# A convolution mixer with seven-product matmuls: the small sums of f's weights on GpSimd behind the next pair's sums, the convolution's second step behind an addition, one Silu a product later

## The chip, the cores and the metric

The kernel runs on one core of one Trainium2 chip. The metric is the device time of one execution in microseconds (us); lower is better. The kernel before took 827.8 us (median of 3 runs, 826.64 to 828.01).

## What is computed

The reference is one layer (DEPTH is 1) of a streaming encoder with a gated short-convolution mixer. The input x is 1024 tokens by 1024 channels in float32, the inner width is 2048.

```python
def short_conv_mixer(u, w_in, conv_w, w_out):
    z, bg, cg, v = jnp.split(u @ w_in.astype(u.dtype), 4, axis=-1)
    y = bg * causal_dwconv(cg * v, conv_w) * jax.nn.silu(z)
    return y @ w_out.astype(u.dtype)
...
    u = rms_norm(h, pre_norm[i])
    m = short_conv_mixer(u, ...)
    h = h + rms_norm(m, post_norm[i])
```

`w_in` is 1024 x 8192 (four blocks of 2048 columns: z, bg, cg, v), the convolution is causal with 3 taps for each channel, `w_out` is 2048 x 1024. The SSD mixer of the reference's file is not used at this depth.

## The kernel before, in words

**The work and its order.** The inner width is cut into 16 chunks of 128 channels (`c`, 0 to 15). A chunk has two pairs of weight blocks: pair 2c is (cg, v), pair 2c+1 is (z, bg). For one pair the projection of all 1024 tokens is a 2 x 2 block product (two weight blocks by two halves of the tokens, and the contraction in two halves), and it is done with seven products `a` to `g` in the place of eight, on sums and differences of the weights (`add_s`: the sums `se`, `sc`, `sf` and, in place, d's; GpSimd) and of the activations (`UH`, `UL`). Each fp32 operand is split into a high and a low part (`wah` and `wal` for the weights of a), and each product is three matmuls for each of four blocks of the contraction: 12 matmuls of 128 x 512. The high part is a copy on ScalarE, the low part a subtraction on VectorE; `split_by_bank` lets ScalarE put a second copy of the source in a PSUM bank (`beside`) and VectorE read that one.

From chunk 3 on product b, and in the chunks 4 to 14 (`by_seven("f", c)`) product f as well, are themselves done by seven smaller products of 128 x 256 (`a'` to `g'`) over both pairs of the chunk at once. Their weights are sums again: `deep_sums(z, c, part)` makes four steps of 128 x 256 in two pages (`dsf0`: lines L730 and L731, `dsf1`: lines L733 and L734 for f; `dsb` for b). `dwf1h`, `dwf1l` are the split parts of `dsf0`, `dwf2h`, `dwf2l` those of `dsf1`.

The products of a chunk of 4 to 14 stand in this order (`slots`): for the even pair c, e, then a', b' of b, d, then a', b' of f, a of the odd pair, c', e' of b, g of the even pair; for the odd pair c, c' and e' of f, e, then f' of b, f' of f, d' of b, d' of f, d, g' of b, g' of f, a of the next chunk's even pair, and last g. TensorE's c adds to the PSUM bank in which a stands, g to the one in which d was added; so c waits until a was copied out of the bank (`snap`, L229, ScalarE), and g until d was added to a page (L248, VectorE).

**What follows a product** is emitted right behind it (`after`, `deep_after`, `deep_after_f`), and `prepare` splits weights about 7 us ahead of their product by a list of nominal times. Each engine runs its instructions in the order in which they were emitted; a step that waits holds up all that stand behind it on its engine. Pages for weights, sums and snapped results come from one ring of 36.

**The convolution** of a chunk starts when d' of b has been added (L783): the gate's product into `gpad` (L271, VectorE), the first tap on ScalarE (L655, into `cv`), the second and the third tap on VectorE (`conv_tap`, L661). After the odd pair's d, `sne` (L248) gets the third part of its sum, and GpSimd multiplies it by the second half of `cv` (L252). After g' of b the page `sna` of the odd pair goes through Silu (L1007, ScalarE), and the Silu of `snc` (L798) follows g' of f. After the odd pair's g VectorE multiplies the first half of `cv` by the bank and by `sna` (L264, L265), and SyncE writes `cv` to DRAM (`y_d`).

**Beside these** VectorE makes sums for the second projection: `add_t` on `w_out` (L342 and L329 to L337, chunks 4 to 11) and `add_y` on finished chunks (L294 in chunks up to 8; from chunk 9 on L299 to L301, which read an earlier chunk that SyncE fetches back, `s<-y_d`). SyncE issues all these DMAs in one queue.

Of the kernel before, what the change touches and what calls it, by code (L numbers as in the profile page):

```python
# [23 lines left out]
def kernel(  # L24
# [16 lines left out]
    nc = tc.nc  # L41
# [194 lines left out]
    def after(p, i):  # L236
# [9 lines left out]
        elif i == "d":  # L246
            t = sn[p, "e"]
            nc.vector.tensor_add(t, x_, t)  # L248
            if p == len(PAIRS) - 1:
                conv_tap(c, TAPS - 1)  # L250
# [18 lines left out]

    def start_conv(c, beside=lambda: None):  # L270
        nc.vector.tensor_mul(gpad[:, TAPS - 1 : TAPS - 1 + HB], banks[2 * c, "x"], sn[2 * c, "a"])  # L271
        conv(c, beside)
# [378 lines left out]

    def conv(c, beside=lambda: None):
        cv = tmp.tile([P, L], F32, tag="cv", name=f"cv_{c}")
        cvs[c] = cv
        nc.scalar.activation(cv, gpad[:, :L], AF.Copy, scale=tap(c, 0))  # L655
        beside()
        for j in range(1, TAPS - (c == NC - 1)):
            conv_tap(c, j)
# [64 lines left out]
    def deep_sums(z, c, part):  # L723

        eng = nc.gpsimd if z == "b" else nc.vector
        (a11, a12), (a21, a22) = rows_of(z, c)
        t = page(f"ds{z}{part}_{c}")
        deep[z, c, part] = t
        if part == 0:
            eng.tensor_add(t[:, :HH], a21, a22)  # L730
            eng.tensor_sub(t[:, HH:], t[:, :HH], a11)  # L731
        else:
            eng.tensor_sub(t[:, :HH], a11, a21)  # L733
            eng.tensor_sub(t[:, HH:], a12, deep[z, c, 0][:, HH:])  # L734
# [45 lines left out]
    def deep_after(c, i):  # L780
        which, row, half = DEEP_C[i]
        t = sn[2 * c + row, "a"][:, half * HH : (half + 1) * HH]
        nc.vector.tensor_add(t, banks[c, "b" + which][:, :HH], t)  # L783
        if i == "d'":
            start_conv(c, lambda: third_unit(1) if c == NC - 1 else None)

    def deep_after_f(c, i):
# [14 lines left out]
        if i == "d'":  # L802
            both = t1.rearrange("p (a b) -> p a b", a=2)
            nc.vector.tensor_add(both, ps.unsqueeze(1).broadcast_to([P, 2, HH]), both)
            return
# [187 lines left out]
    for n, slot in enumerate(slots):  # L993
        if slot[2:]:
# [7 lines left out]
            if i == "e'" and by_seven("f", c):  # L1002
                deep_sums("f", c, 1)
            elif (i, c) == ("f'", NC - 1):
                third_unit(0)
            elif i == "g'":
# [4 lines left out]
        if i == "a" and p % 2 and f7:  # L1011
            deep_sums("f", p // 2, 0)
# [16 lines left out]
        elif i == "e":  # L1029
            add_s(q, "ecdf" if f7 else "ec")  # L1030
            if p % 2 and q in TODO:
# [19 lines left out]
        elif i == "a":  # L1051
            if p % 2 and p in TODO:
                add_t(TODO[p], [2, 3])
# [262 lines left out]
```

## Time and profile before

| | |
|---|---|
| three runs | 826.64, 827.8, 828.01 us |
| the profiled execution | 826.64 us, its span 824.8 us |
| granted TensorE clock, mean | 0.989 |
| TensorE (PE) busy | 783.6 us, 95% |
| VectorE (DVE) busy | 696.9 us, 84% |
| ScalarE (ACT) busy | 400.5 us, 49% |
| GpSimd (POOL) busy | 354.1 us, 43% |

The profile is of one execution. Rows of the timeline give the start, the duration, the engine, the line, what is written and read, and in brackets how long the engine had been idle before and what ended that; where VectorE's steps follow each other directly, the next starts some 0.07 us before the shown end of the last. Rows of the waits read: engine, waiting line, releaser, us in total, how often, the longest. The chunks 4 to 14 lie between about 155 and 650 us of the span: 238 to 360 us are chunks 5 to 7, 500 to 650 us chunks 12 to 14.

### The profile page before, as it was taken

What the parts mean: (1) busy time and instruction counts of PE and PEld (TensorE: products, weight loads), DVE (VectorE), ACT (ScalarE), POOL (GpSimd) and SP (SyncE); (2) the same over time, 40 slices, a digit from 0 to 9 for tenths busy, and PEclk for the clock granted to TensorE, in tenths of its full rate; (3) what the DMA queues carried; (4) which work ended last, traced back from release to release, by engine and by line L of the source; (5) the groups of instructions that cost most, each with busy time, mean ns of one, the idle gap of its engine ahead of it and who ended that gap; (6) DMA issues with size and microseconds to landing.
All of it is one profiled execution on the core that took longest, in us unless ns stands there. A gap on an engine that the chain in (4) does not pass through costs nothing.

```text
span 824.8 us, 11904 instructions
## 1 busy us (share of the span) xinstructions
PE 783.6 (95%) x4050; PEld 665.1 (81%) x4050; DVE 696.9 (84%) x1008; ACT 400.5 (49%) x742; POOL 354.1 (43%) x293
## 2 busy tenths in 40 slices
PE   8999999998999999999897989999999999999997
PEld 7888888887877777778686877888888889988985
DVE  6899658879898989898888888788888899996875
ACT  7654435353535353535263434545554556855730
POOL 2425679685444444444333352535454310430031
PEclk9999999998999999999999999999999999999999
DMA  9112240625162626262737363414141979876445
GB/s 317 42 51 73 68 140 1 192 73 176 57 217 87 221 85 219 85 219 87 228 103 237 115 199 102 141 52 141 52 141 52 314 272 361 303 248 212 153 147 186
DMA packets 115822, 127.18 MB, mean 154 GB/s; under 512 B 7416, under 2 KB 74032, under 8 KB 115760
## 3 DMA queue, kind: packets, MB, share of 16 engines
q1 hardware_dynamic: 115744, 126.41, 47.3%
q8 instruction: 32, 0.52, 0.3%
q14 instruction: 30, 0.25, 0.1%
q10 hardware_dynamic: 16, 0.00, 0.0%
HBM read 91.78 MB, written 34.60 MB: 153 GB/s over the span
## 4 chain that ended last, share of the span: by engine, by line
PE 37%; DVE 20%; issue 8%; ACT 5%; DMA 3%; POOL 1%; DVEq 0%; POOLq 0%; SPq 0%; ACTq 0%
PE px L221 4%; PE po_x L1105 4%; PE po_x L1107 4%; PE po_x L1106 4%; PE px L222 3%; PE px L223 3%; DMA s<-y_d 3%; ACT beside L182 1%; DVE t L342 1%; DVE sne L248 1%; DVE dsf L734 1%; DVE sna L783 1%; DVE snc L807 1%; PE pv L222 1%; PE pv L221 1%
## 5 line engine op out<-in xcount | busy, mean ns | idle before, releaser
L252 POOL TENSOR_TENSOR sne<-sne,cv 128x512 f32<-128x512 f32 x15 | 20.9, 1396 | 153.1 <-DVE sne L248 137.9
L221 PE MATMUL px<-u_c,wcl 128*128 128x512 f32 x124 | 52.1, 420 | 20.6 <-ACT sna L229 20.6
L661 DVE SCALAR_TENSOR_TENSOR cv<-gpad,cw,cv 128x1024 f32<-128x1024 f32 x32 | 42.8, 1338 | 18.4 <-ACT cv L655 17.8
L152 POOL TENSOR_TENSOR se<-raw,raw 128x512 f32<-128x512 f32 x31 | 44.1, 1422 | 31.1 <-DVE t L334 12.8
L221 PE MATMUL px<-u_g,wgl 128*128 128x512 f32 x124 | 49.7, 401 | 5.9 <-DVE sne L248 5.9
L187 DVE TENSOR_TENSOR wel<-se,weh 128x512 fp32r<-128x512 f32 x31 | 37.6, 1213 | 19.1 <-ACT weh L168 19.1
L182 ACT COPY beside<-raw 128x512 f32<-128x512 f32 x66 | 38.9, 590 | 30.0 <-DVE dwf0l L183 14.5
L222 PE MATMUL px<-u_c,wch 128*128 128x512 f32 x124 | 51.0, 411 | 0.0
L223 PE MATMUL px<-u_c,wch 128*128 128x512 f32 x124 | 51.0, 411 | 0.0
L154 POOL TENSOR_TENSOR sc<-se,raw 128x512 f32<-128x512 f32 x31 | 46.6, 1503 | 8.4 <-POOL se L152 4.1
L156 POOL TENSOR_TENSOR sf<-raw,sc 128x512 f32<-128x512 f32 x31 | 48.6, 1567 | 1.8 <-DVE dsf L734 1.0
L221 PE MATMUL px<-u_d,wdl 128*128 128x512 f32 x124 | 48.6, 392 | 0.0
L221 PE MATMUL px<-u_a,wal 128*128 128x512 f32 x124 | 48.6, 392 | 0.0
L222 PE MATMUL px<-u_g,wgh 128*128 128x512 f32 x124 | 48.5, 392 | 0.0
L222 PE MATMUL px<-u_a,wah 128*128 128x512 f32 x124 | 48.5, 391 | 0.0
L222 PE MATMUL px<-u_d,wdh 128*128 128x512 f32 x124 | 48.5, 391 | 0.0
L222 PE MATMUL pv<-u_e,weh 128*128 128x512 f32 x124 | 48.4, 390 | 0.0
L223 PE MATMUL px<-u_d,wdh 128*128 128x512 f32 x124 | 48.4, 390 | 0.0
L221 PE MATMUL pv<-u_e,wel 128*128 128x512 f32 x124 | 48.4, 390 | 0.0
L223 PE MATMUL px<-u_g,wgh 128*128 128x512 f32 x124 | 48.3, 389 | 0.0
L223 PE MATMUL pv<-u_e,weh 128*128 128x512 f32 x124 | 48.3, 389 | 0.0
L221 PEld LDWEIGHTS px<-u_c,wcl 128*128 128x128 f32 x124 | 24.8, 200 | 29.1 <-ACT sna L229 24.0
(534 smaller groups left out, 2741.3 us busy)
## 6 DMA issues: line engine op xcount, KB each, us to landing
raw<-in_sc_w_in SPq DMA_DIRECT2D x128, 256.0 KB, 4.3
y_d<-cv SPq DMA_DIRECT2D x16, 512.0 KB, 2.9
s_d<-s SPq DMA_DIRECT2D x32, 256.0 KB, 4.5
t<-in_sc_w_out SPq DMA_DIRECT2D x32, 256.0 KB, 3.2
t_d<-t SPq DMA_DIRECT2D x32, 256.0 KB, 2.4
tb<-in_sc_w_out SPq DMA_DIRECT2D x16, 256.0 KB, 4.0
s<-y_d SPq DMA_DIRECT2D x16, 256.0 KB, 4.6
xr<-in_x SPq DMA_DIRECT2D x16, 256.0 KB, 4.5
```

The source lines that it names most:

```text
L152: nc.gpsimd.tensor_add(t, block(p, 1, 0), block(p, 1, 1))
L154: nc.gpsimd.tensor_sub(t, sums[p, "e"], block(p, 0, 0))
L156: nc.gpsimd.tensor_sub(t, block(p, 0, 1), sums[p, "c"])
L182: nc.scalar.copy(b, src)
L187: nc.vector.tensor_sub(lo, source(p, i), hi.bitcast(F32))
L221: nc.tensor.matmul(ps, lo, UH[i][:, k], start=first and k == 0, stop=False, skip_group_check=True)
L222: nc.tensor.matmul(ps, hi, UL[i][:, k], start=False, stop=False, skip_group_check=True)
L223: nc.tensor.matmul(ps, hi, UH[i][:, k], start=False, stop=last, skip_group_check=True)
L661: nc.vector.scalar_tensor_tensor(cvs[c], gpad[:, j : j + L], tap(c, j), cvs[c], op0=ALU.mult, op1=ALU.add)
L1105: nc.tensor.matmul(ps, lo, u[:, 0, k], start=first, stop=False, skip_group_check=True)
L1106: nc.tensor.matmul(ps, hi, u[:, 1, k], start=False, stop=False, skip_group_check=True)
L1107: nc.tensor.matmul(ps, hi, u[:, 0, k], start=False, stop=last, skip_group_check=True)
```

## The change

Three edits and what follows from the first, all for the chunks 4 to 14:

1. `deep_sums` for f runs on GpSimd, as for b, and both parts stand behind e of the even pair, right behind the sums of the odd pair's weights (`add_s(q, "ecdf")`). Before, part 0 stood ahead of the odd pair's a, part 1 behind e' of b, both on VectorE.
2. The convolution is cut up. Behind d' of b stand the gate's product and the first tap only; the second tap follows the addition of d' of f, and the third tap the addition of the odd pair's d (L248).
3. The Silu of `sna` moves from behind g' of b to behind a of the next chunk (after the snap of that a).
4. Since the pages of `dsf0` and `dsf1` are taken from the ring earlier, the pages behind them shift by two places.

```diff
--- before.py
+++ after.py
@@ -246,7 +246,7 @@
         elif i == "d":
             t = sn[p, "e"]
             nc.vector.tensor_add(t, x_, t)
-            if p == len(PAIRS) - 1:
+            if p == len(PAIRS) - 1 or p % 2 and by_seven("f", c):
                 conv_tap(c, TAPS - 1)
             if p % 2:
                 nc.gpsimd.tensor_mul(t, t, cvs[c][:, HB:])
@@ -267,8 +267,11 @@
             elif c < DEEP:
                 start_conv(c)
 
+    def gate(c):
+        nc.vector.tensor_mul(gpad[:, TAPS - 1 : TAPS - 1 + HB], banks[2 * c, "x"], sn[2 * c, "a"])
+
     def start_conv(c, beside=lambda: None):
-        nc.vector.tensor_mul(gpad[:, TAPS - 1 : TAPS - 1 + HB], banks[2 * c, "x"], sn[2 * c, "a"])
+        gate(c)
         conv(c, beside)
 
 
@@ -649,10 +652,12 @@
     add_s(2, "ecdf")
     fetch(3)
 
+    def first_tap(c):
+        cvs[c] = tmp.tile([P, L], F32, tag="cv", name=f"cv_{c}")
+        nc.scalar.activation(cvs[c], gpad[:, :L], AF.Copy, scale=tap(c, 0))
+
     def conv(c, beside=lambda: None):
-        cv = tmp.tile([P, L], F32, tag="cv", name=f"cv_{c}")
-        cvs[c] = cv
-        nc.scalar.activation(cv, gpad[:, :L], AF.Copy, scale=tap(c, 0))
+        first_tap(c)
         beside()
         for j in range(1, TAPS - (c == NC - 1)):
             conv_tap(c, j)
@@ -722,16 +727,15 @@
 
     def deep_sums(z, c, part):
 
-        eng = nc.gpsimd if z == "b" else nc.vector
         (a11, a12), (a21, a22) = rows_of(z, c)
         t = page(f"ds{z}{part}_{c}")
         deep[z, c, part] = t
         if part == 0:
-            eng.tensor_add(t[:, :HH], a21, a22)
-            eng.tensor_sub(t[:, HH:], t[:, :HH], a11)
+            nc.gpsimd.tensor_add(t[:, :HH], a21, a22)
+            nc.gpsimd.tensor_sub(t[:, HH:], t[:, :HH], a11)
         else:
-            eng.tensor_sub(t[:, :HH], a11, a21)
-            eng.tensor_sub(t[:, HH:], a12, deep[z, c, 0][:, HH:])
+            nc.gpsimd.tensor_sub(t[:, :HH], a11, a21)
+            nc.gpsimd.tensor_sub(t[:, HH:], a12, deep[z, c, 0][:, HH:])
 
 
     DEEP_W = {"a'": (0, 0), "b'": (0, HH), "e'": (1, 0), "c'": (1, HH), "d'": (2, 0), "f'": (2, HH), "g'": (3, 0)}
@@ -782,7 +786,11 @@
         t = sn[2 * c + row, "a"][:, half * HH : (half + 1) * HH]
         nc.vector.tensor_add(t, banks[c, "b" + which][:, :HH], t)
         if i == "d'":
-            start_conv(c, lambda: third_unit(1) if c == NC - 1 else None)
+            if by_seven("f", c):
+                gate(c)
+                first_tap(c)
+            else:
+                start_conv(c, lambda: third_unit(1) if c == NC - 1 else None)
 
     def deep_after_f(c, i):
 
@@ -802,6 +810,7 @@
         if i == "d'":
             both = t1.rearrange("p (a b) -> p a b", a=2)
             nc.vector.tensor_add(both, ps.unsqueeze(1).broadcast_to([P, 2, HH]), both)
+            conv_tap(c, 1)
             return
         t = (t1 if i == "e'" else t0)[:, slice(0, HH) if i == "a'" else slice(HH, HB)]
         nc.vector.tensor_add(t, ps, t)
@@ -999,17 +1008,13 @@
                 deep_after_f(c, i)
                 continue
             deep_after(c, i)
-            if i == "e'" and by_seven("f", c):
-                deep_sums("f", c, 1)
-            elif (i, c) == ("f'", NC - 1):
+            if (i, c) == ("f'", NC - 1):
                 third_unit(0)
-            elif i == "g'":
+            elif i == "g'" and not by_seven("f", c):
                 nc.scalar.activation(sn[2 * c + 1, "a"], sn[2 * c + 1, "a"], AF.Silu)
             continue
         i, p = slot
         f7 = by_seven("f", p // 2)
-        if i == "a" and p % 2 and f7:
-            deep_sums("f", p // 2, 0)
         product(p, i)
         prepare(n)
         after(p, i)
@@ -1028,6 +1033,9 @@
                 deep_sums("b", p // 2, 1)
         elif i == "e":
             add_s(q, "ecdf" if f7 else "ec")
+            if f7 and p % 2 == 0:
+                for part in (0, 1):
+                    deep_sums("f", p // 2, part)
             if p % 2 and q in TODO:
                 fetch_t(TODO[q])
             elif p in TODO and p % 2 == 0:
@@ -1049,6 +1057,8 @@
             if p % 2 and q <= END and q // 2 >= DEEP:
                 deep_sums("b", q // 2, 0)
         elif i == "a":
+            if prev >= 0 and p % 2 == 0 and by_seven("f", prev):
+                nc.scalar.activation(sn[p - 1, "a"], sn[p - 1, "a"], AF.Silu)
             if p % 2 and p in TODO:
                 add_t(TODO[p], [2, 3])
         if DEEP < NC and (i, p) in UNDER:
```

The order of the instructions in three places follows; in the rows of the changed kernel the line numbers are its own (L666 there is L661 here, L802 is L794, L812 is L804, L787 is L783, L806 is L798, L1061 is L1007, L734 to L738 are L730 to L734). Names end in pair or chunk and a buffer's number: `snc_13` is of pair 13, the odd one of chunk 6.

VectorE at the convolution of chunk 6, before:

```order
L271 TENSOR_TENSOR gpad_624<-px_12_2459,sna_12_2476 128x512
L661 SCALAR_TENSOR_TENSOR cv_6_2806<-gpad_624,cw_77,cv_6_2806 128x1024 x2
L183 TENSOR_TENSOR wgl_13_2817<-beside_1546,wgh_13_2816 128x512
L804 TENSOR_TENSOR snc_13_2721<-px2f_6_2621,snc_13_2721 128x512
L187 TENSOR_TENSOR wcl_14_2835<-sc_14_2765,wch_14_2834 128x512
L248 TENSOR_TENSOR sne_13_2761<-px_13_2644,sne_13_2761 128x512
L783 TENSOR_TENSOR sna_13_2661<-px2b_6_2567,sna_13_2661 128x256
L794 TENSOR_TENSOR snc_13_2721<-pv_13_2742,snc_13_2721 128x512
```

and with the change:

```order
L271 TENSOR_TENSOR gpad_624<-px_12_2458,sna_12_2475 128x512
L183 TENSOR_TENSOR wgl_13_2815<-beside_1546,wgh_13_2814 128x512
L812 TENSOR_TENSOR snc_13_2721<-px2f_6_2627,snc_13_2721 128x512
L666 SCALAR_TENSOR_TENSOR cv_6_2806<-gpad_624,cw_77,cv_6_2806 128x1024
L187 TENSOR_TENSOR wcl_14_2834<-sc_14_2765,wch_14_2833 128x512
L248 TENSOR_TENSOR sne_13_2761<-px_13_2647,sne_13_2761 128x512
L666 SCALAR_TENSOR_TENSOR cv_6_2806<-gpad_624,cw_77,cv_6_2806 128x1024
L787 TENSOR_TENSOR sna_13_2664<-px2b_6_2573,sna_13_2664 128x256
L802 TENSOR_TENSOR snc_13_2721<-pv_13_2742,snc_13_2721 128x512
```

`wgl_13` and `snc_13` stand ahead of the first of VectorE's two taps now, and the second one stands between the additions to `sne_13` and to `snc_13`.

ScalarE at the same place, before:

```order
L655 ACTIVATE cv_6_2806<-gpad_624,cw_77 128x1024
L181 CAST wgh_13_2816<-raw_13_11_2440 128x512
L182 COPY beside_1546<-raw_13_11_2440 128x512
L168 CAST wch_14_2834<-sc_14_2765 128x512
L1007 ACTIVATE sna_13_2661<-sna_13_2661 128x512
L798 ACTIVATE snc_13_2721<-snc_13_2721 128x512
L168 CAST weh_14_2878<-se_14_2763 128x512
L229 COPY sna_14_2882<-px_14_2865 128x512
L181 CAST dwb0h_7_2896<-raw_14_01_2608 128x512
```

and with the change:

```order
L657 ACTIVATE cv_6_2806<-gpad_624,cw_77 128x1024
L181 CAST wgh_13_2814<-raw_13_11_2440 128x512
L182 COPY beside_1546<-raw_13_11_2440 128x512
L168 CAST wch_14_2833<-sc_14_2765 128x512
L806 ACTIVATE snc_13_2721<-snc_13_2721 128x512
L168 CAST weh_14_2877<-se_14_2763 128x512
L229 COPY sna_14_2881<-px_14_2864 128x512
L1061 ACTIVATE sna_13_2664<-sna_13_2664 128x512
L181 CAST dwb0h_7_2896<-raw_14_01_2614 128x512
```

The Silu of `sna_13` has gone from ahead of `weh_14` and of the copy of `sna_14` to behind them; the first tap still stands ahead of the two copies for `wgl_13`.

VectorE behind the even pair's wcl_13 of chunk 6, before (the steps of `dsf1_6` follow six rows after `dwf1l_6`):

```order
L187 TENSOR_TENSOR wcl_13_2636<-sc_13_2558,wch_13_2635 128x512
L794 TENSOR_TENSOR snc_12_2523<-pv_12_2536,snc_12_2523 128x512
L730 TENSOR_TENSOR dsf0_6_2641<-sf_13_2561 128x256
L731 TENSOR_TENSOR dsf0_6_2641<-dsf0_6_2641,sf_12_2362 128x256
L161 TENSOR_TENSOR dwf1l_6_2658<-dsf0_6_2641,dwf1h_6_2657 128x512
L334 TENSOR_TENSOR t23_10_2614<-t23_10_2614,tb0_10_2529 128x256
```

with the change:

```order
L187 TENSOR_TENSOR wcl_13_2642<-sc_13_2558,wch_13_2641 128x512
L802 TENSOR_TENSOR snc_12_2523<-pv_12_2536,snc_12_2523 128x512
L161 TENSOR_TENSOR dwf1l_6_2661<-dsf0_6_2563,dwf1h_6_2660 128x512
L337 TENSOR_TENSOR t23_10_2620<-t23_10_2620,tb0_10_2529 128x256
L340 TENSOR_TENSOR tb1_10_2530<-tb1_10_2530,t23_10_2620 128x256
```

and GpSimd, where the four steps stand now:

```order
L156 TENSOR_TENSOR sf_13_2561<-raw_13_01_2436,sc_13_2558 128x512
L734 TENSOR_TENSOR dsf0_6_2563<-sf_13_2561 128x256
L735 TENSOR_TENSOR dsf0_6_2563<-dsf0_6_2563,sf_12_2362 128x256
L737 TENSOR_TENSOR dsf1_6_2566<-sf_12_2362,sf_13_2561 128x256
L738 TENSOR_TENSOR dsf1_6_2566<-sf_12_2362,dsf0_6_2563 128x256
L804 TENSOR_TENSOR gpad_624<-snc_12_2523,sne_12_2554 128x256
L152 TENSOR_TENSOR se_14_2763<-raw_14_10_2616,raw_14_11_2618 128x512
```

Before, the row of `gpad` followed that of `sf_13` directly on GpSimd. The four steps are gone from VectorE and stand on GpSimd ahead of the even pair's `gpad`.

## The prediction

> **What bounds the kernel now.** I read the page's busy times first, then the waits of all engines, then the busy times by stretch, and last the timelines of VectorE, ScalarE, TensorE and GpSimd in chunk 7, which is a plain one. The page and the waits (engine and line that wait, releaser, total, how often, longest):
>
> ```profile
> span 824.8 us, 11904 instructions
> PE 783.6 (95%) x4050; PEld 665.1 (81%) x4050; DVE 696.9 (84%) x1008; ACT 400.5 (49%) x742; POOL 354.1 (43%) x293
> ...
> PE px L221 <- ACT sna L229: 20.6, 8, 4.9
> PE px L221 <- DVE sne L248: 5.9, 11, 1.0
> ACT dwf1h L160 <- DVE dsf L731: 68.4, 11, 8.8
> ```
>
> TensorE is busy 95% of the span, but it does wait: 20.6 us in 8 chunks ahead of c, whose bank ScalarE has yet to copy. Ahead of that copy on ScalarE stands the cast of `dwf1h`, which waits in all 11 chunks for VectorE's `dsf0`. Now the stretches, each from one odd c to the next (length; then PE, PEld, DVE, ACT and POOL busy with their counts; the granted clock; the DMAs' share and GB/s):
>
> ```profile
> 197.00:202.40 5.40, 5.40 (x13) 4.24 (x14) 5.40 (x13) 2.81 (x7) 1.28 (x1) 0.50 0.33 121
> 321.80:362.80 41.00, 38.42 (x204) 32.27 (x204) 36.49 (x54) 19.00 (x36) 18.59 (x15) 1.00 0.47 151
> 451.90:496.60 44.70, 39.56 (x204) 33.48 (x204) 37.88 (x56) 19.11 (x36) 18.63 (x15) 0.96 0.50 161
> 575.50:614.00 38.50, 37.77 (x206) 32.35 (x205) 32.67 (x48) 19.03 (x35) 17.89 (x15) 1.00 0.34 103
> ```
>
> The first is only the 5.4 us behind a long wait (3.2 us, chunk 4): there the granted clock is 0.50. The chunks 5 to 11 take 41 to 45 us with VectorE busy 36.5 to 37.9, the chunks 12 to 14 take 38.5 with 32.7, and TensorE's own work is alike. So two limits lie close together: VectorE's row of instructions, whose waits fill the rest of its 41 us, sets chunks 4 to 11, and TensorE's row of products, at 38.5, the last three. VectorE between the two pairs, with ScalarE and TensorE:
>
> ```profile
> 319.23 0.42 DVE L730 TENSOR_TENSOR dsf<-sf 128x256 f32<-128x256 f32 x1
> 319.69 0.84 DVE L731 TENSOR_TENSOR dsf<-dsf,sf 128x256 f32<-128x256 f32 x1
> 321.27 0.69 DVE L161 TENSOR_TENSOR dwf1l<-dsf,dwf1h 128x512 fp32r<-128x512 f32 x1 [0.74 <-ACT dwf1h L160]
> 324.59 1.44 DVE L733 TENSOR_TENSOR dsf<-sf,sf 128x256 f32<-128x256 f32 x1
> 325.96 1.51 DVE L734 TENSOR_TENSOR dsf<-sf,dsf 128x256 f32<-128x256 f32 x1
> 327.39 1.78 DVE L161 TENSOR_TENSOR dwb2l<-dsb,dwb2h 128x512 fp32r<-128x512 f32 x1
> 329.10 0.68 DVE L161 TENSOR_TENSOR dwf2l<-dsf,dwf2h 128x512 fp32r<-128x512 f32 x1
> ```
> ```profile
> 320.62 0.62 ACT L160 CAST dwf1h<-dsf 128x512 fp32r<-128x512 f32 x1 [5.00 <-DVE dsf L731]
> 321.14 0.58 ACT L229 COPY sna<-px 128x512 f32<-128x512 f32 x1
> ```
> ```profile
> 321.77 0.50 PE L221 MATMUL px<-u_c,wcl 128*128 128x512 f32 x1 [1.14 <-ACT sna L229]
> 496.61 0.80 PE L221 MATMUL px<-u_c,wcl 128*128 128x512 f32 x1 [4.22 <-ACT sna L229]
> ```
>
> The reader sees the whole loop: VectorE's two steps, the cast, the copy, and c 1.14 us late; at the end of chunk 11 it is 4.22 us.
>
> **The change part by part.** *A, the sums leave VectorE.* `dsf0` with the wait for its cast runs from 319.23 to 321.27, 2.04 us; `dsf1` from 324.59 to 327.39, 2.80 us: 4.84 us, the bound from above. Not all of it stays: the operations behind slide forward into GpSimd's own sums. The same form takes 0.42 (L730) and 0.84 (L731) or 1.5 (L734) here, and `dwb2l` 1.78 where `dwf2l` takes 0.68. If three or four 512-wide steps slide into such neighbours I lose 0.5 us with each, about 1.5 in all (an estimate). The bound from below: what slides in pays what the steps there pay now, 2.1 (L733 and L734 over two free steps) and once more the 1.1 of `dwb2l` over `dwf2l`, which leaves 1.6. I take 4.84 - 1.5 = 3.3, between the two.
>
> *B, the sums come to GpSimd,* behind `sf` and ahead of the even pair's `gpad`, beside VectorE's second L342 pair:
>
> ```profile
> 349.37 2.88 DVE L342 TENSOR_TENSOR t<-t,t 128x512 f32<-128x512 f32 x2
> 352.78 1.78 DVE L342 TENSOR_TENSOR t<-t,t 128x512 f32<-128x512 f32 x2
> 184.42 1.82 DVE L342 TENSOR_TENSOR t<-t,t 128x512 f32<-128x512 f32 x2
> ```
> ```profile
> 184.46 1.24 POOL L734 TENSOR_TENSOR dsb<-raw,dsb 128x256 f32<-128x256 f32 x1
> 319.40 0.85 POOL L796 TENSOR_TENSOR gpad<-snc,sne 128x256 f32<-128x256 f32 x1 [7.04 <-DVE snc L794]
> ```
>
> The pair took 1.82 us when it started with such a small step (184.42 and 184.46), 1.78 at its present place, 2.88 beside 512-wide sums. I take +0.05, with +1.1 as the end above. Four steps of at most 1.24 us fill 5 us on GpSimd, and the next in its row, `gpad`, waits 7.04 us for VectorE anyhow: no one is late, and if that cover were gone `gpad` would be late by the remainder. `dsf0` is ready some 25 us before its cast, so the cast and the copy of `sna` no longer wait for it.
>
> Weighed against the Trainium skill (page "SBUF — State Buffer", section "Who interferes with whom"): there VectorE and GpSimd share a pair of ports under an exclusive lock, and a VectorE instruction with two SBUF inputs contends with GpSimd's reads. The 1.44 against 0.42 above agrees that such neighbours cost, while the 1.82 beside a small step does not look like a lock held for whole steps. By the lock B would cost 1.1 instead of 0.05, and it is a rival below.
>
> *C, the convolution's second tap goes behind d' of f.* `wgl` then stands directly behind the gate:
>
> ```profile
> 334.45 1.16 ACT L655 ACTIVATE cv<-gpad,cw 128x1024 f32<-128x1024 f32 x1 [3.21 <-issue]
> 336.02 0.58 ACT L182 COPY beside<-raw 128x512 f32<-128x512 f32 x1
> 335.64 2.61 DVE L661 SCALAR_TENSOR_TENSOR cv<-gpad,cw,cv 128x1024 f32<-128x1024 f32 x2 [1.27 <-ACT cv L655]
> 338.16 0.69 DVE L183 TENSOR_TENSOR wgl<-beside,wgh 128x512 fp32r<-128x512 f32 x1
> ```
>
> The gate ends at 335.64 - 1.27 = 334.37. Before, VectorE waited 1.27 us for the first tap; now the next thing it does needs `beside`, which on ScalarE still stands behind that tap and ends at 336.60: a wait of 2.23 us, +0.95. Queued behind it are the additions to `snc`, the tap, `wcl`, `sne` (L248): all move with it. Two taps are as long apart as together (2.61). It is worth 0 only if something else is late, and at most the 2.23. I take +1.0.
>
> *D, the Silu of `sna`* leaves the place ahead of `weh` and comes behind the copy of the next `sna`, ahead of the cast for `dwb0`. It takes 0.63 us like its neighbour, the Silu of `snc` below, so `dwb0l` on VectorE is up to 0.6 late; the copy loses a step ahead of it. Bounds 0 and +0.63; I take +0.6.
>
> *E, the third tap between L248 and the addition to `snc`.* g is released by L248, so it does not feel this; the next chunk's c does, through ScalarE:
>
> ```profile
> 340.89 0.69 DVE L794 TENSOR_TENSOR snc<-pv,snc 128x512 f32<-128x512 f32 x1
> 341.61 0.63 ACT L798 ACTIVATE snc<-snc 128x512 f32<-128x512 f32 x1
> 342.65 0.58 ACT L229 COPY sna<-px 128x512 f32<-128x512 f32 x1
> ...
> 554.58 0.50 PE L221 MATMUL px<-u_g,wgl 128*128 128x512 f32 x1 [0.34 <-DVE sne L248]
> 557.43 0.39 PE L221 MATMUL px<-u_c,wcl 128*128 128x512 f32 x1
> ```
>
> From the end of L248 the tap takes 1.3, the addition of 256 columns 0.4, that to `snc` 0.7 (about 2.25 with the overlaps of 0.07); from the end of L794 (341.58) to that of the copy (343.23) it is 1.65 us: 3.9 in all. g starts with the end of L248 and lasts 2.85 (554.58 to 557.43, where the next c follows it without a gap), so that c waits some 1.1 us for the copy, in all 11 chunks. Where TensorE's row sets the time, that is a loss; against it stands up to 0.25 of the 0.34 that g waits for L248, which has one tap fewer ahead of it. Net +0.9 in each of chunks 12 to 14; bounds 0 (the addition early) and +1.2.
>
> *F, the ring.* `raw` of the next pair waits for a page two places later, and SyncE's one queue with it. A fetch asked for one product (2.85 us) later is needed only by sums a third of a chunk later: 0, bounded by +0.5 a chunk if it isn't.
>
> **The sum** in VectorE's row is -3.3 + 0.05 + 1.0 + 0.6 = -1.65 a chunk, 41.0 to 39.4; TensorE's is 38.5 + 0.9 = 39.4, so the two meet and neither hides much of the other. Chunks 5 to 8 and the step to 9: four times -1.6 = -6.4. In chunks 9 and 10, where a fetched page and a copy are waited for,
>
> ```profile
> 445.75 0.69 DVE L299 TENSOR_TENSOR s<-s,cv 128x512 f32<-128x512 f32 x1 [2.22 <-DMA s<-y_d]
> 416.89 0.69 DVE L183 TENSOR_TENSOR wal<-beside,wah 128x512 fp32r<-128x512 f32 x1 [0.52 <-ACT beside L182]
> ```
>
> the wait for the page stays and the 0.52 for `beside` goes with the cast: -2.1 twice, -4.2. Into chunk 12: -1.6 and about half of the 2.7 us (5.4 at clock 0.50) that the slow clock costs behind a wait of 4.2: -2.9. Into chunk 5, where VectorE has less to do: -0.5 (0 to -1.6). Chunks 12 to 14: 3 x 0.9 = +2.7. Together -11.3: the profiled execution's 826.64 would become 815.3; the median of the runs, 827.8, lies 1.2 above it: **816.5 us**.
>
> **The rivals.** *R1, the slack is kept:* nothing is given back in A and the wait of E doesn't form, since the addition to `snc` is early. Then TensorE's 38.5 bounds every chunk: 7 chunks with 0.9 less and no +2.7, near 807. The busy VectorE rows at 1.4 to 1.8 us speak against it. *R2, the pair of steps is held:* the second L342 pair takes 2.88 as beside 512-wide sums; +1.05 in 7 chunks, less some 2 us that the DMA waits of chunks 9 to 11 take up: 822. For it stands 349.37, against it 184.42. (It is what the Trainium skill's section above would make of B.) *R3, slower:* VectorE's relief in A is eaten by GpSimd's steps in their new place and by sliding. At a relief of 1.6 C and D alone eat it, and if E's 1.1 comes into VectorE's row too (its additions wait for TensorE's late products), a chunk becomes 1.1 longer: 826.64 + 7 x 1.1 + 2.7 - 1.4 (slow clock) = 836, against the runs' median 837. It decides from a relief under about 2.9, where 7 chunks and those 1.3 us cancel. A's bound from below allows it; that `dwf1h` alone frees 2.04 speaks against. *R4, no change:* gains and costs cancel near that 2.9, 828.
>
> **How the numbers follow.** Likeliest 0.60, R1 0.09, R2 0.15, R3 0.10, R4 0.06. The likeliest's own range is 810 to 821 (A's bounds, halved, over 8 chunks). The range of 8 in 10 goes from 806 (R1) to 827 (R2, and R4's nearer part), and leaves out R3. A measurement here tells 0.2%, 1.7 us, from no change: faster is the likeliest, R1 and R2 less 0.02 for their tails, 0.82; within it R4 and a tail, 0.07; slower 0.11.
>
> **What would show it.** Right: GpSimd has the 11 x 4 rows of `dsf`; ScalarE's wait for `dsf` is gone; TensorE's wait of the odd c for `sna` is gone up to chunk 8; a new one of about 1.1 stands at the even c in 11 chunks; VectorE waits 2.2 for `beside` ahead of `wgl` and up to 0.6 ahead of `dwb0l`; a chunk takes 39.4, in 5 to 8 and in 12 to 14 alike. R2 shows as L342 at 2.9 twice a chunk, R3 as chunks over 41 us with VectorE's rows of 1.4 us multiplied. The prediction is wrong if VectorE's row doesn't shorten by 1 to 2 us, or if TensorE waits somewhere new, for `wgl` or for a page of `raw`.

## The result

The changed kernel takes 818.5 us (median of 5 runs, 817.9 to 818.9) against 828.0 us before (5 runs, 826.6 to 828.7): ratio 0.9887, 95% interval 0.9872 to 0.9901, so 1.1% less. The forecast was 816.5 us in a range of 806 to 827. Its profiled execution took 818.51 us, 8.1 less than that of before, and so did its span (816.7 against 824.8).

Of the profile after, first the page's busy times and the waits of all engines (engine and line that wait, releaser, total, how often, longest). L-numbers are now those of the changed kernel: L666 is the second and third tap, L802 the addition to `snc` at the odd pair's e and at g' of f, L816 another addition to `snc`, L735 a step of `dsf`.

```profile
PE 780.3 (96%) x4050; PEld 663.9 (81%) x4050; DVE 675.2 (83%) x964; ACT 399.6 (49%) x742; POOL 401.9 (49%) x337
...
DVE wgl L183 <- ACT beside L182: 28.5, 22, 2.3
PE pv2f L780 <- DVE snc L816: 10.3, 7, 2.6
PE px L221 <- DVE wcl L187: 6.7, 4, 2.3
PE px L221 <- ACT sna L229: 6.0, 8, 0.8
ACT dwf1h L160 <- POOL dsf L735: 5.9, 4, 4.1
PE px L221 <- DVE sne L248: 2.7, 6, 0.7
```

The 44 steps of `dsf` are on GpSimd (293 instructions have become 337, VectorE's 1008 are 964). TensorE's wait of 20.6 us for `sna` ahead of the odd c is gone. Three smaller ones stand in its place: `pv2f` (f's small products) waits 10.3 us for VectorE where it was 4.5 before, the odd c 6.7 us in the chunks 4, 9, 10 and 11 for `wcl`, and the even c 6.0 us for `sna` in 8 chunks, the wait that the forecast had from the third tap's place. VectorE's new wait ahead of `wgl` is there, too.

The stretches that answer to the four of before (length; PE, PEld, DVE, ACT, POOL busy with counts; granted clock; DMA share; GB/s): the start behind the odd c of chunk 4, then chunks 7, 10 and 13 from odd c to odd c.

```profile
196.40:201.80 5.40, 4.74 (x26) 4.06 (x27) 5.40 (x10) 3.04 (x8) 3.40 (x3) 1.00 0.38 126
318.25:358.25 40.00, 38.14 (x206) 32.38 (x205) 34.76 (x51) 18.98 (x35) 23.14 (x20) 1.00 0.49 153
442.60:485.20 42.60, 38.46 (x204) 32.31 (x205) 36.29 (x52) 18.97 (x35) 22.93 (x19) 1.00 0.51 161
566.10:605.45 39.35, 37.91 (x206) 32.33 (x205) 29.32 (x44) 19.06 (x35) 21.93 (x20) 1.00 0.33 101
```

By the starts of c, chunk 7 is 1.1 shorter (41.05 to 39.99), chunk 10 2.1, and chunk 13 is 0.75 longer (38.60 to 39.35), although VectorE has 3.3 us less to do in it. The whole, from the starts of the odd c in the two traces:

| stretch | before, us | after, us | difference | forecast |
|---|---|---|---|---|
| start to chunk 4 | 196.98 | 196.41 | -0.57 | 0 |
| 4 to 5 | 42.71 | 42.71 | 0.00 | -0.5 |
| 5 to 9 | 166.77 | 159.85 | -6.92 | -6.4 |
| 9 to 11 | 90.15 | 86.25 | -3.90 | -4.2 |
| 11 to 12 | 40.19 | 41.51 | +1.32 | -2.9 |
| 12 to 15 | 116.87 | 118.82 | +1.95 | +2.7 |
| chunk 15 to the end | 171.13 | 171.15 | +0.02 | 0 |
| sum | 824.8 | 816.7 | -8.1 | -11.3 |

The rows that carry it, VectorE first, then GpSimd, then TensorE (start, us, ..., idle before and releaser):

```profile
332.62 0.69 DVE L183 TENSOR_TENSOR wgl<-beside,wgh 128x512 fp32r<-128x512 f32 x1 [2.26 <-ACT beside L182]
341.70 0.69 DVE L183 TENSOR_TENSOR dwb0l<-beside,dwb0h 128x512 fp32r<-128x512 f32 x1 [0.64 <-POOL dsb L734]
344.37 1.30 DVE L265 TENSOR_TENSOR cv<-cv,sna 128x512 f32<-128x512 f32 x1
349.61 2.32 DVE L345 TENSOR_TENSOR t<-t,t 128x512 f32<-128x512 f32 x2
360.74 1.45 DVE L161 TENSOR_TENSOR dwb2l<-dsb,dwb2h 128x512 fp32r<-128x512 f32 x1
362.11 1.78 DVE L161 TENSOR_TENSOR dwf2l<-dsf,dwf2h 128x512 fp32r<-128x512 f32 x1
363.81 1.78 DVE L187 TENSOR_TENSOR wdl<-raw,wdh 128x512 fp32r<-128x512 f32 x1
```
```profile
343.83 1.29 POOL L152 TENSOR_TENSOR se<-raw,raw 128x512 f32<-128x512 f32 x1
...
350.31 1.07 POOL L734 TENSOR_TENSOR dsf<-sf 128x256 f32<-128x256 f32 x1
351.46 1.07 POOL L735 TENSOR_TENSOR dsf<-dsf,sf 128x256 f32<-128x256 f32 x1
...
359.84 1.79 POOL L152 TENSOR_TENSOR se<-raw,raw 128x512 f32<-128x512 f32 x1 [0.92 <-DMA raw<-in_sc_w_in]
361.71 1.63 POOL L154 TENSOR_TENSOR sc<-se,raw 128x512 f32<-128x512 f32 x1
363.30 1.74 POOL L148 TENSOR_TENSOR raw<-raw,raw 128x512 f32<-128x512 f32 x1
```
```profile
340.13 0.50 PE L221 MATMUL px<-u_c,wcl 128*128 128x512 f32 x1 [0.76 <-ACT sna L229]
485.22 0.47 PE L221 MATMUL px<-u_c,wcl 128*128 128x512 f32 x1 [1.43 <-DVE wcl L187]
495.14 0.39 PE L780 MATMUL pv2f<-u_f,dwf2l 128*128 128x256 f32 x1 [1.97 <-DVE snc L816]
544.18 0.50 PE L221 MATMUL px<-u_g,wgl 128*128 128x512 f32 x1 [0.67 <-DVE sne L248]
```

The reader is to see three things. `wgl` waits 2.26 us (2.2 was forecast). The second pair of `t` sums (L345, before L342) takes 2.32 us beside the new steps on GpSimd where it took 1.78. And `dwf2l` and `wdl`, which took 0.68 each before, have slid beside GpSimd's 512-wide sums and take 1.78 each: that is the relief given back, and `pv2f`, which needs the addition behind them, is late by it.

### The profile page after: what moved, and what is told of

Its sections match the earlier page's. It is cut to its first block, busy times and chain, and to the rows that moved or that the text cites. A ratio compares the mean times of both kernels' runs of the same rounds, so it can differ in the third digit from the quotient of the medians.

```text
span 816.7 us, 11954 instructions
## 1 busy us (share of the span) xinstructions
PE 780.3 (96%) x4050; PEld 663.9 (81%) x4050; DVE 675.2 (83%) x964; ACT 399.6 (49%) x742; POOL 401.9 (49%) x337
## 4 chain that ended last, share of the span: by engine, by line
PE 62%; DVE 19%; issue 9%; POOL 4%; ACT 4%; DMA 3%; DVEq 0%; POOLq 0%; SPq 0%; ACTq 0%
PE px L221 8%; PE px L222 7%; PE px L223 7%; PE po_x L1115 4%; PE po_x L1116 4%; PE po_x L1117 4%; PE pv L221 3%; PE pv L223 3%; PE pv L222 3%; DVE cv L666 3%; DMA s<-y_d 2%; DVE t L345 1%; ACT beside L182 1%; DVE sna L787 1%; DVE wel L187 1%
## 5 line engine op out<-in xcount | busy, mean ns | idle before, releaser
L221 PE MATMUL px<-u_c,wcl 128*128 128x512 f32 x124 | 49.7, 401 | 12.8 <-DVE wcl L187 6.7
L187 DVE TENSOR_TENSOR wel<-se,weh 128x512 fp32r<-128x512 f32 x31 | 37.0, 1193 | 19.1 <-ACT weh L168 19.1
L229 ACT COPY snc<-px 128x512 f32<-128x512 f32 x31 | 18.2, 586 | 69.7 <-PE px L223 69.7
L154 POOL TENSOR_TENSOR sc<-se,raw 128x512 f32<-128x512 f32 x31 | 49.5, 1596 | 2.6 <-POOL se L152 0.2
L148 POOL TENSOR_TENSOR raw<-raw,raw 128x512 f32<-128x512 f32 x31 | 49.3, 1590 | 0.0
L223 PE MATMUL px<-u_c,wch 128*128 128x512 f32 x124 | 48.4, 390 | 0.0
L222 PE MATMUL px<-u_c,wch 128*128 128x512 f32 x124 | 48.3, 389 | 0.0
```

The costliest lines, as they stand in the source:

```text
L148: nc.gpsimd.tensor_sub(t, block(p, 0, 0), t)
L154: nc.gpsimd.tensor_sub(t, sums[p, "e"], block(p, 0, 0))
L187: nc.vector.tensor_sub(lo, source(p, i), hi.bitcast(F32))
L221: nc.tensor.matmul(ps, lo, UH[i][:, k], start=first and k == 0, stop=False, skip_group_check=True)
L222: nc.tensor.matmul(ps, hi, UL[i][:, k], start=False, stop=False, skip_group_check=True)
L223: nc.tensor.matmul(ps, hi, UH[i][:, k], start=False, stop=last, skip_group_check=True)
```

## Experiments

Twelve kernels, each timed in 5 rounds against the kernel before on the same chip. The first four take the change apart.

**Only the sums** (the changed kernel with convolution and Silu as before):

```diff
-            if p == len(PAIRS) - 1 or p % 2 and by_seven("f", c):
+            if p == len(PAIRS) - 1:
...
-            if by_seven("f", c):
-                gate(c)
-                first_tap(c)
-            else:
-                start_conv(...)
+            start_conv(...)
...
-            conv_tap(c, 1)
...
-            elif i == "g'" and not by_seven("f", c):
+            elif i == "g'":
...
-            if prev >= 0 and p % 2 == 0 and by_seven("f", prev):
-                nc.scalar.activation(sn[p - 1, "a"], sn[p - 1, "a"], AF.Silu)
```

> Only the four sums of f's weights are on GpSimd; convolution and Silu stand as before. T1 (each edit has its own price on VectorE's row or TensorE's: in chunk 7 of the two traces the sums free 4.84 - 2.06 given back - 0.54 for the slower L342 pair = 2.24 us, and the convolution and the Silu cost 0.84 together): the plain chunk goes from 41.05 to 38.8, chunks 12 to 14 stay at 38.5, about 811 us, 7 us below the changed kernel. T2 (the edits need each other: without the cut convolution VectorE's freed time only turns into a later wait, and the sums alone are worth no more than the whole change): 817 to 822 us. T3 (the sums alone do not pay, the convolution does): 825 or more.

Measured: 811.0 us (810.2 to 811.4), ratio 0.9795 (0.9778 to 0.9812). T1 to the microsecond: the sums alone are worth 17 us, nearly twice what the whole change brings. Odd c to odd c the chunks 12 and 13 stay at 38.6.

**Only the convolution** (sums on VectorE, Silu as before; the first three hunks above stay as in the change):

> Only the convolution is cut up; the sums are on VectorE and the Silu at its place before. T1: VectorE waits 2.2 us ahead of wgl for the copy beside it and loses 0.9 us a chunk in chunks 4 to 11; in 12 to 14 the even c waits for ScalarE's copy of sna, with the Silu ahead of it about 1.3 us: 7 x 0.9 + 4 x 1.2 = +11, about 839 us. T2: the cut is worth something or nothing by itself, 824 to 829 us.

Measured: 836.8 us (836.0 to 838.0), ratio 1.0109 (1.0092 to 1.0125). The cut convolution costs 8.8 us; T2 is out. From its waits, TensorE:

```profile
PE px L221 <- ACT sna L229: 29.7, 19, 4.9
```

Nineteen waits where there were 8: the even c now waits 0.72 to 0.77 in each of the 11 chunks beside the odd ones of before. T1 had 1.3 there and 839 us; that size was wrong, as the next run shows.

**The Silu of `sna` back** behind g' of b (only the last two hunks above):

> The changed kernel with the Silu of sna back behind g' of b: sums and convolution changed. T1: ScalarE's copy of the next pair's sna stands one Silu (0.54 us) later, so the even c waits about 1.3 us where it waited 0.75, in all 11 chunks; VectorE's dwb0l is 0.5 earlier. Chunks 12 to 14 pay 0.5 each, the plain chunks, where both rows are close, 0 to 0.5: 819.5 to 823 us. T2 (the Silu's place costs VectorE 0.5 a chunk and gives nothing): 814 to 816 us.

Measured: 818.2 us (817.8 to 818.8), ratio 0.9883 (0.9866 to 0.99): neither, the Silu's place is worth nothing. Its rows, chunk 7, VectorE and GpSimd:

```profile
341.47 0.69 DVE L183 TENSOR_TENSOR dwb0l<-beside,dwb0h 128x512 fp32r<-128x512 f32 x1
...
344.14 1.82 DVE L265 TENSOR_TENSOR cv<-cv,sna 128x512 f32<-128x512 f32 x1
```
```profile
344.13 1.28 POOL L152 TENSOR_TENSOR se<-raw,raw 128x512 f32<-128x512 f32 x1
```

Two things cancel. On ScalarE the Silu fits into the wait for the addition to `snc`, so the copy of the next `sna` is no later (the even c still waits 0.75 to 0.77 in 8 chunks). On VectorE `dwb0l` is 0.5 earlier: from the gate's start (L271 at 329.96 here, 329.67 in the changed kernel) it is 11.51 us against 12.03. But L265 takes 1.82 in the place of 1.30, and the next step starts 15.93 us behind the gate in both. L265 ends 0.55 us behind GpSimd's `se` in both (345.96 and 345.41; 345.67 and 345.12): an earlier start only waits longer.

**The convolution back**, sums and Silu changed (the first three hunks above):

> The changed kernel with the convolution as before, sums on GpSimd and the Silu a product later. T1: without the wait of 2.2 us ahead of wgl and without the third tap behind L248 the even c waits for nothing, chunks 12 to 14 return to 38.5, the plain chunk to 38.8 to 39.3: 811 to 814 us. T2 (the cut convolution is what lets the sums pay): 818 us or more.

Measured: 811.5 us (809.9 to 812.3), ratio 0.98 (0.9781 to 0.9819). T1. The parts add up: sums -17.1 and convolution +8.8 give -8.3, the whole change -9.5, within 1.2 us of each other; the Silu is nothing by this or the run before.

**The first tap behind the copies.** The next three runs ask what the convolution's cost consists of. In the first, only ScalarE's order is changed:

```diff
             if by_seven("f", c):
                 gate(c)
-                first_tap(c)
...
             nc.vector.tensor_add(both, ps.unsqueeze(1).broadcast_to([P, 2, HH]), both)
+            first_tap(c)
             conv_tap(c, 1)
```

> The changed kernel with the first tap moved on ScalarE behind the two copies for wgl (it is emitted behind d' of f, right ahead of the second tap). T1 (the wait of 2.26 us on VectorE ahead of wgl is the copy standing behind the first tap): that wait is gone in 11 chunks, VectorE's row of a plain chunk falls from 39.7 below TensorE's, which is left with the even c's wait of 0.75: a chunk takes 38.9 to 39.1, 812 to 815 us. T2 (VectorE's wait is slack, or comes back ahead of the second tap): 817 to 819 us.

Measured: 797.2 us (797.0 to 798.3), ratio 0.9639 (0.9626 to 0.9652). In the direction of T1, and four times its size. ScalarE and VectorE in chunk 7, then its stretch of chunk 13, odd c to odd c:

```profile
322.83 0.59 ACT L182 COPY beside<-raw 128x512 f32<-128x512 f32 x1 [0.84 <-DVE wal L183]
324.93 1.16 ACT L657 ACTIVATE cv<-gpad,cw 128x1024 f32<-128x1024 f32 x1 [1.51 <-DVE gpad L271]
```
```profile
324.76 0.68 DVE L183 TENSOR_TENSOR wgl<-beside,wgh 128x512 fp32r<-128x512 f32 x1
...
326.12 1.28 DVE L666 SCALAR_TENSOR_TENSOR cv<-gpad,cw,cv 128x1024 f32<-128x1024 f32 x1
```
```profile
548.10:585.45 37.35, 37.35 (x206) 32.50 (x205) 29.33 (x44) 19.16 (x35) 22.02 (x20) 1.00 0.34 106
```

The copies do not need the gate; placed ahead of the tap they run in the time in which ScalarE waits for it. VectorE waits for neither. With L248 two microseconds earlier both the wait of g for it and that of the even c vanish (what is left of 0.25 us or more in the chunks 4 to 14 is `pv2f`, 8.5 us in 7 chunks, and the odd c, 5.0 us in 4): TensorE works without a gap in chunk 13, 37.35 of 37.35. My expectation had taken 38.5 for TensorE's own time in a chunk. It was not: of the 38.5 it was busy for 37.77 before, and the rest was g waiting for L248 (0.34 and 0.45 us in chunks 12 and 13) and `pv2f` for an addition, both on VectorE.

**Both at once: the third tap ahead of L248 as well**

```diff
-                first_tap(c)
...
+            first_tap(c)
             conv_tap(c, 1)
+            conv_tap(c, 2)
...
-            if p == len(PAIRS) - 1 or p % 2 and by_seven("f", c):
+            if p == len(PAIRS) - 1:
```

> As the run before, and the third tap right behind the second, ahead of the odd d's addition. T1 (the even c's wait is the third tap between L248 and the addition to snc; in the gap that the 2.26 us leave, the third tap fits ahead of L248): the even c waits for nothing, g waits its 0.3, TensorE's row of a chunk 38.0 to 38.6: 805 to 809 us, below the kernel with the sums alone (811). T2 (two taps ahead of L248 make g late by a tap): 812 to 818 us.

Measured: 798.4 us (796.5 to 800.5), ratio 0.9651 (0.9635 to 0.9667): the same as the run before, and below both expectations, which stood on the 38.5. With VectorE on time the place of the third tap is free.

**The third tap ahead of L248, the first still ahead of the copies** (the hunks above without those on `first_tap`)

> The changed kernel with the third tap right behind the second, the first tap still ahead of the copies for wgl. T1: the even c's wait of 0.75 is gone, but L248 comes a tap (1.2 us) later and g waits for it 1.5 to 1.9 us: chunks 12 to 14 lose 0.4, the plain ones the same or less: 819 to 823 us. T2 (the even c's wait has another cause): the wait of 0.75 stays beside the late g, 826 or more.

Measured: 823.8 us (822.1 to 825.1), ratio 0.9954 (0.9942 to 0.9967), 5 more than the changed kernel. From its waits:

```profile
PE px L221 <- DVE sne L248: 14.6, 10, 2.0
```

No wait for `sna` of 0.25 us or more is left at the even c, as T1 says: it came from the third tap behind L248. In its place g waits, 1.5 to 2.0 us in chunks 12 to 14. Behind two of these waits the granted clock is 0.50 for 3.41 us, so that 3.4 us of the loss in the profiled execution are the clock's (the last section shows how).

**Without the four steps.** The split parts are made from the pages of `sf`, so f's small products have other weights, and what the kernel returns is not the layer:

```diff
-            src = deep[z, c, n - 1] if n else ...
+            src = sums[2 * c + n - 1, "f"] if z == "f" and n else deep[z, c, n - 1] if n else ...
...
-            if f7 and p % 2 == 0:
-                for part in (0, 1):
-                    deep_sums("f", p // 2, part)
```

> The changed kernel without the four steps of dsf: the split parts of dsf0 and dsf1 are made from the two pages of sf instead, so f's small products have other weights. It prices the steps on GpSimd. T1 (they cost what the second L342 pair shows, 2.32 against 1.78 us): that pair is at 1.8 again, 0.5 us a chunk in chunks 4 to 11, 813.5 to 816 us. T2 (hidden: TensorE's row takes over at once): 817 to 819. T3 (they also cause the slow steps behind dwf1l, 2 us a chunk, given back in my sum): 808 or less; by T1 and T2 those steps stay slow, beside the 512-wide sums.

Measured: 814.6 us (813.3 to 815.0), ratio 0.9842 (0.9829 to 0.9856). The second pair in chunk 7, and the two slow steps:

```profile
346.81 1.78 DVE L345 TENSOR_TENSOR t<-t,t 128x512 f32<-128x512 f32 x2
...
359.56 1.78 DVE L161 TENSOR_TENSOR dwf2l<-sf,dwf2h 128x512 fp32r<-128x512 f32 x1
361.26 1.77 DVE L187 TENSOR_TENSOR wdl<-raw,wdh 128x512 fp32r<-128x512 f32 x1
```

The steps cost some 3.7 us (0.9887 less 0.9842 of the time before), but only a part of it as T1 has it: the pair is back at 1.78, yet a plain chunk gains no more than 0.3 (gate to gate 39.46 for 39.66 in chunk 7). The greatest piece, 1.9 us, comes up to the gate of chunk 4. T3 is out: `dwf2l` and `wdl` are as slow without the steps; what they run into is GpSimd's ordinary sums. For chunk 4 these rows say why, three of the changed kernel and one of this run:

```profile
193.84 0.62 ACT L160 CAST dwf1h<-dsf 128x512 fp32r<-128x512 f32 x1 [4.08 <-POOL dsf L735]
193.13 1.82 DVE L161 TENSOR_TENSOR ufel_deep<-deepf,ufeh_deep 128x256 fp32r<-128x256 f32 x2
195.57 0.69 DVE L187 TENSOR_TENSOR wcl<-sc,wch 128x512 fp32r<-128x512 f32 x1 [0.29 <-POOL dsf L738]
```
```profile
192.41 0.75 DVE L161 TENSOR_TENSOR ufel_deep<-deepf,ufeh_deep 128x256 fp32r<-128x256 f32 x2
```

There GpSimd has a backlog (the first chunk of f's seven products), and `dsf0` holds its cast up for 4.1 us. What ends c's wait, though, is `wcl` on VectorE, not ScalarE's copy: VectorE runs beside the late steps and is slowed by them, `ufel_deep` by 1.07 us and the sum L297 ahead of it by 0.54 (1.22 us for 0.68).

**Three on the better kernel, and one on the kernel before.** First the Silu back in the kernel with the copies first (the hunks as above):

> The kernel of copies_first (797.2 us) with the Silu of sna back behind g' of b. T1 (the Silu runs in ScalarE's wait of 4 to 5 us for the addition to snc, and what it makes dwb0l late, 0.5 us, comes back at L265, which ends when GpSimd's sum beside it ends): 796 to 799 us, no difference, L265 at about 1.8 us in the place of 1.3. T2 (its 0.5 us a chunk counts once the wait ahead of wgl is gone): 791 to 794 us.

Measured: 796.8 us (796.1 to 797.3), ratio 0.9623 (0.9609 to 0.9637), no difference, and L265 takes 1.85 us in chunk 7 where it took 1.32: T1.

The kernel before, with nothing else changed than the convolution's start:

```diff
         if i == "d'":
-            start_conv(...)
+            if by_seven("f", c):
+                nc.vector.tensor_mul(gpad[...], banks[2 * c, "x"], sn[2 * c, "a"])
+            else:
+                start_conv(...)
...
             nc.vector.tensor_add(both, ps.unsqueeze(1).broadcast_to([P, 2, HH]), both)
+            conv(c)
```

> The kernel before, and only the first tap (with both others right behind it) moved behind wgl's two copies and the addition of d' of f; sums on VectorE, taps together, Silu as before. T1 (the order on ScalarE is what counts, and it is worth the 1.27 us that VectorE waited for the first tap in every chunk, with the wait of g for L248): 1.3 a chunk in 4 to 11, about 1 in 12 to 14: 812 to 817 us. T2 (before the change that wait was covered by the cast of dwf1h and the late c): 825 to 828 us.

Measured: 815.8 us (814.8 to 816.7), ratio 0.9853 (0.9837 to 0.9868): the size of T1. Before the change too, 12 us lay in where the taps stand. How much of it is ScalarE's order alone this run does not show, since VectorE's two taps moved with it, behind `wgl` and the addition to `snc`.

The sums of chunk 4 on VectorE, as before, in the kernel with the copies first:

```diff
+        eng = nc.vector if (z, c) == ("f", DEEP_F) else nc.gpsimd
...
+            if (i, c) == ("e'", DEEP_F):
+                deep_sums("f", c, 1)
...
+        if i == "a" and p == 2 * DEEP_F + 1:
+            deep_sums("f", DEEP_F, 0)
...
-            if f7 and p % 2 == 0:
+            if f7 and p % 2 == 0 and p // 2 > DEEP_F:
```

> The kernel of copies_first with the sums of chunk 4 alone on VectorE, at the places of before. T1 (chunk 4 has a backlog on GpSimd, so that dwf1h waits 4.1 us for dsf0 there and the odd c 2.3 us; without any sums this chunk took 1.9 us less): the wait for GpSimd is gone, but the one for VectorE (3.2 us before) comes back with the 2 to 5 us of sums: 796 to 799 us. T2 (VectorE has the time in chunk 4): 795 or less.

Measured: 798.7 us (796.6 to 799.5), ratio 0.964 (0.9623 to 0.9657): nothing gained, as T1 says: the odd c of chunk 4 waits 3.2 us for `sna` again, where it waited 2.3 for `wcl`. The lateness of chunk 4 can be moved from one engine to the other, not removed in this way.

Last, the Silu of `snc` and the product behind it behind the next copy of `sna`, in the kernel with the copies first:

```diff
-            else:
-                nc.scalar.activation(t, t, AF.Silu)
-                nc.gpsimd.tensor_mul(cvs[c][:, HB:], t, sn[p + 1, "e"])
...
             if prev >= 0 and p % 2 == 0 and by_seven("f", prev):
+                t = sn[p - 1, "c"]
+                nc.scalar.activation(t, t, AF.Silu)
+                nc.gpsimd.tensor_mul(cvs[prev][:, HB:], t, sn[p - 1, "e"])
                 nc.scalar.activation(sn[p - 1, "a"], sn[p - 1, "a"], AF.Silu)
```

> The kernel of copies_first with the Silu of snc, and GpSimd's product behind it, also moved behind the copy of the next sna. T1 (VectorE's wait of 1.2 us ahead of wel is weh standing behind that Silu on ScalarE): that wait is gone in 11 chunks; VectorE's row is near TensorE's by now, so a plain chunk gains 0 to 1: 787 to 796 us. T2 (TensorE's own products bound, VectorE's wait is slack): 796 to 799 us; slower if GpSimd's product and the sums of dsb behind it become late.

Measured: 791.4 us (790.0 to 792.5), ratio 0.9558 (0.9541 to 0.9574), the fastest of all and within T1. Its chunk 7, odd c to odd c, and VectorE's wait for `weh`, 19.1 us in all before and in the changed kernel:

```profile
311.95:349.30 37.35, 37.35 (x205) 32.51 (x204) 34.36 (x51) 19.33 (x35) 22.79 (x19) 1.00 0.52 166
```
```profile
DVE wel L187 <- ACT weh L168: 5.8, 4, 2.6
```

In this stretch TensorE has no gap, with VectorE at 34.4 of 37.35 us: from here a plain chunk is TensorE's. In the chunks 9 to 11 `pv2f` still waits 0.9 to 2.0 us for VectorE.

## Why the prediction was right, and where it was not

The time, 818.5 for 816.5, and the sign came out by the likeliest case. That the sum of a plain chunk came within 0.3 us is in part luck: A and B were too good by 0.5 each, and D, which came to nothing, was too dear by 0.6. Its terms for a plain chunk, from gate to gate in chunk 7 of both traces (41.05 and 39.66 us):

| term | forecast | measured | from |
|---|---|---|---|
| A, sums off VectorE | -3.3 | -2.8 | 4.84 freed, 2.06 given back |
| B, second pair beside the steps | +0.05 | +0.54 | 2.32 for 1.78 |
| C, wait ahead of `wgl` and taps apart | +1.0 | +0.87 | addition to `snc` 8.08 us behind the gate for 7.21 |
| D, Silu | +0.6 | 0.0 | `dwb0l` +0.52, L265 -0.55 |
| sum | -1.65 | -1.4 | |

- *A* held, within its bounds. What is given back is `dwf2l` and `wdl` (1.10 each), L337 (0.54) and `dwb` (0.44), less 0.78 at `wel` and 0.33 at `dwb2l`; I had 1.5 for 2.06. The runs show that this is GpSimd's ordinary sums (`dwf2l` and `wdl` stay slow without the four steps).
- *B* was mis-sized, at the argument against R2. I read the pair of 1.82 us as not being held for whole steps. It is held, and the prediction's own rows say so: that pair ends at 186.24, 0.54 us behind the end of the small GpSimd step (184.46 + 1.24 = 185.70). In the same way, above, `dwb2l` ends at 362.19, `dwf2l` at 363.89 and `wdl` at 365.59, each 0.55 to 0.56 us behind the end of a GpSimd sum (361.63, 363.34, 365.04); the second of the pair ends at 351.93, 0.55 behind a `dsf` step (351.38). The price of a neighbour is the rest of its instruction: 0.54 us for a step of 256 columns here, 1.10 for one of 512. This is the exclusive lock of the Trainium skill (page "SBUF — State Buffer", section "Who interferes with whom"); the traces agree with it. B lies between the prediction's two prices, 0.05 and 1.1.
- Also in *B*, "ready some 25 us before its cast" was wrong: `dsf0` ends at 352.53 (351.46 + 1.07) and ScalarE begins its cast at 353.94, 1.4 us later. In a plain chunk that is enough; in chunk 4 it was not, and the cast waits 4.08 us.
- *C* and its reason, the copy behind the first tap, were right in place and size (2.26 us for 2.23). It is the costliest part of the change: the copies' order alone is worth about 20 us (0.9639 against 0.9887 of the time before).
- *D* was wrong: "`dwb0l` on VectorE is up to 0.6 late" is true (0.52), but the lateness ended at the next step that GpSimd held anyway.
- *E* was right that the even c would wait: 0.75 us for 1.1, in 8 of the 11 chunks. That g "does not feel this" is right of the third tap, but the credit of 0.25 was not: g waits 0.67 in chunks 12 and 13 for 0.34 and 0.45 before, and only in chunk 14 no longer. Chunks 12 to 14 lost 1.95 for 2.7.
- *F*, the ring, was priced by no run of its own. GpSimd's wait for `raw` ahead of `se` grew from 3.5 to 6.3 us; the sums alone, which have the same ring, came out at 811.0 for an expected 811 without a term for it.
- *Chunk 11 to 12* is the step that failed: forecast -2.9, measured +1.32, a miss of 4.2 where the whole span missed by 3.2. The forecast took off 1.6 for VectorE's shorter row and 1.3 for the slow clock. The first had little to take: before, TensorE waited for VectorE in this stretch only 0.71 us, at g (the odd c's wait, 4.22 before and 1.43 now, lies in the stretch 9 to 11). The second came to nothing: a new wait of 1.97 us stands at `pv2f` 10 us behind that c, since `dwf2l` and `wdl` take 1.77 and 1.76 there, and the clock falls behind it as it fell behind the old one (0.68 over the next 5.4 us, 0.71 before). I had named those steps as the give-back on VectorE and not asked which product needs what comes behind them. The slow clock was also priced too high: 2.7 us was chunk 4's, and 0.71 over 5.4 us is 1.6. The other misses are small: +0.5 (4 to 5), -0.5 (5 to 9), +0.3 (9 to 11), -0.75 (12 to 15) and -0.57 ahead of chunk 4, whose odd c waits 2.26 us for 3.18.
- *The frame was wrong where it did no harm.* "TensorE's row of products, at 38.5" bounds nothing: TensorE needs 37.35 us, and VectorE set the last chunks as well. In the sum of the chunks 12 to 14 this cost nothing, as E's wait hangs on L248 and so on VectorE; in my expectation for the run with the copies first it cost 15 us.

Of the rivals, R1 (no give-back) fell by the slow steps, R3 and R4 by the sums' 17 us. R2 had the right mechanism for B and too high a price, since the second step only meets a short neighbour.

## What to carry to other kernels

On an engine that works in order, ask of each instruction whether it could have run while the one ahead of it waited: two copies that needed nothing, behind a tap that needed the gate, cost about 20 us here, more than moving 44 instructions to another engine brought. A change of several parts is worth taking apart even where the whole is a gain: this one was a gain of 17 and a loss of 9. And before a stage is called bound by its busiest engine, subtract that engine's small waits and see on whom they hang: 38.5 us with waits of 0.3 to 0.45 us turned out to be 37.35.

## What the hardware showed

**A held VectorE step ends with its neighbour.** A VectorE step of 512 columns with two SBUF operands, which takes 0.68 us alone, ended 0.55 us behind the end of the GpSimd instruction beside it, whether it began 0.01 us behind that one's start (L265 in the run with the Silu back, 1.82 us) or 0.54 behind it (1.30 us). In the changed kernel's trace this holds within 0.01 us for 147 of the 150 such steps that took over 0.8 us beside a GpSimd instruction already under way. So on VectorE up to half a microsecond of lateness ahead of such a step cost nothing here, and starting it earlier brought nothing.

**The clock behind a wait depends on where the wait falls.** The granted clock does not follow from the wait's length alone: behind 3.18 us in chunk 4 it was 0.50 over the next 5.4 us before, behind 2.26 us it stayed at 1.00 in the changed kernel, and with the sums only, behind 2.30 us at the same place, it was 0.71. In each of the 14 traces the clock changes only on a grid of 3.41 us, whose place differs from trace to trace. The same wait of 1.97 us at `pv2f` in chunk 11 shows what that does, in windows of this grid, first in the changed kernel, then in the one with the copies first (granted clock is the third number from the end):

```profile
492.09:495.51 3.42, 1.46 (x11) 1.21 (x10) 3.42 (x6) 1.59 (x3) 1.78 (x2) 1.00 0.73 216
495.51:498.92 3.41, 3.41 (x19) 3.41 (x18) 2.95 (x7) 0.00 (x1) 0.00 (x0) 0.50 0.26 76
498.92:502.33 3.41, 3.41 (x19) 2.91 (x19) 1.23 (x3) 2.70 (x4) 0.00 (x0) 1.00 0.00 0
```
```profile
476.90:480.31 3.41, 2.11 (x13) 1.68 (x11) 3.41 (x3) 1.97 (x4) 2.81 (x2) 1.00 0.69 200
480.31:483.72 3.41, 2.74 (x21) 2.65 (x22) 3.38 (x10) 0.76 (x2) 0.00 (x0) 1.00 0.37 110
483.72:487.14 3.42, 3.42 (x21) 3.01 (x20) 3.34 (x5) 1.66 (x2) 0.00 (x0) 1.00 0.00 0
```

In the first the whole wait falls into one window, and the next window runs at 0.50; in the second it is split over two, and nothing follows. Between 150 and 690 us of all 14 traces, of the windows at 1.00, all 36 in which TensorE stood idle for 1.95 us or more were followed by a window at 0.50, none of the 2089 with less than 1.85 us was, and three of the five between were. A window at 0.50 costs TensorE about 1.7 us of work (half of 3.41). The trace of the kernel before has five of them, the changed kernel's three, that of the copies first one, so some 3.4 of the 20 us between the last two are the clock's. The grid's place is luck: a wait of 2 us may cost 2 or 3.7 us. What sets the place no run here shows.
